# A second FFN's gate and up as seven block products, in three phases instead of one

## The chip, the cores and the metric
The kernel runs on one core of one Trainium2 chip. The metric is the device time of one execution in microseconds; less is better. Engines are called TensorE (PE in the profile, its weight loads PEld), VectorE (DVE), ScalarE (ACT), GpSimd (POOL) and SyncE (SP, which issues DMAs).

## The reference, cut to what matters
One layer: a gated FFN, a mixer, a second gated FFN, each behind a norm with a scale and shift that depend on the sequence (1024 prompt tokens and 8 x 4 sample tokens, model width 1024, hidden width 2816, float32).

```python
h = _modulate(_rms(x, p["ffn1_norm"]), sh1, sc1)
x = x + 0.5 * g1[:, None, :] * _swiglu(h, p["ffn1_w_gate"], p["ffn1_w_up"], p["ffn1_w_down"])
h = _modulate(_rms(x, p["mix_norm"]), sh2, sc2)
m, new = _mixer(h, conv[l], hst[l], shift[l], wkv[l], p)
x = x + g2[:, None, :] * m
h = _modulate(_rms(x, p["ffn2_norm"]), sh3, sc3)
x = x + 0.5 * g3[:, None, :] * _swiglu(h, p["ffn2_w_gate"], p["ffn2_w_up"], p["ffn2_w_down"])
y = _rms(x, final_norm)
# _swiglu: (silu(h @ w_gate) * (h @ w_up)) @ w_down
```

## The kernel before, in words
Activations lie transposed: 8 tiles of 128 features (KD) by T = 1056 tokens. Every float32 operand of a product is split into a high and a low part, and `mm3` (lines 61 to 63) adds three matmuls: high x low, low x high, high x high. Tokens go in pieces CH of 384, 384 and 288 columns. The hidden width is 22 tiles of 128.

**The first FFN** has two phases. In the first, tokens are two pairs (528 columns each, halves of 264 or 266), features are two halves, and gate and up are taken together as the two rows of a 2 x 2 block matrix. `Up.pair` forms the four output blocks of one hidden tile and one pair with seven block products instead of eight, each of 4 x 3 matmuls (tiles pX, pY, pZ, pW); the sums of weights (`summed`) and of activations (`Blocks.sums`, `split_sums`, slots t1 to t4) are made before. Hidden tiles 0 and 1 go plainly with eight (`plain_mm`), to give time for the sums. Hidden tiles are stored to DRAM (dh). At its start come the norm (`pair_rstd`, `pair_norm`), the modulation (`ada8`: matmuls adaps; parts 2 to 8 run behind the products), the scale sc1 (`coeff`, line 160) and the splits. There GpSimd does the sums of blocks and the additions of squares of pair 1. In the second phase `ffn` with dH reads hidden tiles back, splits them and multiplies by w_down in groups of 2 or 3 tiles (GROUPS; psum pd), and VectorE adds the result into x (`acc_x`, line 445).

**The mixer** (projections, two recurrences) ends with a chain of 16 chunks (pd, line 973), with other work as filler in between: at last `w_out` (psum po), two halves of the contraction; the first half for all three token pieces, then the second half piece by piece as the chain delivers, each piece followed by the third norm (`norm3`: squares nsq, sums nacc on VectorE, h).

**The second FFN** is one phase: for each group of hidden tiles gate and up plainly (pg, pu: 8 x 3 matmuls on each of three token pieces), silu, split in SBUF, then down (pd); the last group's down ends piece by piece with the final norm.

The order of instructions on each engine comes from a planner with a simulated timeline, except where `in_order` fixes it; a tile's slot is handed on when its last reader is done. One program order, many queues: DMAs wait in the queue of the engine that issues them.

## Time and profile before

| | |
|---|---|
| time, median of 3 runs | 2252.24 us (2249.97 to 2261.13) |
| the profiled execution | 2250.29 us, of which the span is 2248.5 us |
| TensorE busy | 2153.0 us, 96% |
| VectorE busy | 1219.0 us, 54% |
| ScalarE busy | 647.3 us, 29% |
| GpSimd busy | 208.8 us, 9% |
| moved by DMA | 227.8 MB |

The profiled execution is one run; busy is the time in which at least one instruction of the engine runs. Matmuls are pipelined, so the cost of one is the distance between two starts, not its own duration.

### The profile page before, as it was taken

What the parts mean: (1) busy time and instruction counts of PE and PEld (TensorE: products, weight loads), DVE (VectorE), ACT (ScalarE), POOL (GpSimd) and SP (SyncE); (2) the same over time, 40 slices, a digit from 0 to 9 for tenths busy, and PEclk for the clock granted to TensorE, in tenths of its full rate; (3) what the DMA queues carried; (4) which work ended last, traced back from release to release, by engine and by line L of the source; (5) the groups of instructions that cost most, each with busy time, mean ns of one, the idle gap of its engine ahead of it and who ended that gap; (6) DMA issues with size and microseconds to landing.
All of it is one profiled execution on the core that took longest, in us unless ns stands there. A gap on an engine that the chain in (4) does not pass through costs nothing.

```text
span 2248.5 us, 39509 instructions
## 1 busy us (share of the span) xinstructions
PE 2153.0 (96%) x16633; PEld 2040.1 (91%) x16633; DVE 1219.0 (54%) x2511; ACT 647.3 (29%) x1102; POOL 208.8 (9%) x264
## 2 busy tenths in 40 slices
PE   5899999999999989899898889999999999999997
PEld 4799999999999988798786689899999999999997
DVE  5755555565956576674855666853433333232325
ACT  4433232333312144443332442431111111212123
POOL 3300000000000041214220000000000000000004
PEclk8999999999999999999999899999999999999998
DMA  6244444443623121346476666111111111101112
GB/s 229 95 147 151 138 141 144 136 142 106 237 85 107 56 89 51 97 105 149 115 173 160 180 152 141 40 61 45 48 48 48 38 48 38 57 32 63 38 48 78
DMA packets 135666, 227.80 MB, mean 101 GB/s; under 512 B 74080, under 2 KB 90496, under 8 KB 133440
## 3 DMA queue, kind: packets, MB, share of 16 engines
q1 hardware_dynamic: 74336, 155.71, 21.6%
q10 hardware_dynamic: 49488, 35.45, 6.8%
q0 software_dynamic: 11664, 34.11, 5.3%
q8 instruction: 131, 2.15, 0.4%
q14 instruction: 47, 0.39, 0.1%
HBM read 177.55 MB, written 47.60 MB: 100 GB/s over the span
## 4 chain that ended last, share of the span: by engine, by line
PE 83%; DVE 6%; DMA 4%; ACT 3%; issue 2%; ACTq 1%; POOL 0%; SPq 0%; DVEq 0%; POOLq 0%
PE pd L61 7%; PE pd L63 7%; PE pd L62 7%; PE pg L61 4%; PE pu L61 4%; PE pu L62 4%; PE pu L63 4%; PE pg L63 4%; PE pg L62 4%; PE pX L61 2%; PE pZ L61 2%; PE pW L63 2%; PE pW L62 2%; PE pj L61 2%; PE pX L63 2%
## 5 line engine op out<-in xcount | busy, mean ns | idle before, releaser
L63 PE MATMUL pd<-fh,wh 128*128 128x384 f32 (+1 forms) x1056 | 340.8, 323 | 0.0
L62 PE MATMUL pd<-fh,wl 128*128 128x384 f32 (+1 forms) x1056 | 340.4, 322 | 0.0
L61 PE MATMUL pd<-fl,wh 128*128 128x384 f32 (+1 forms) x1056 | 339.1, 323 | 0.0
L47 DVE TENSOR_TENSOR wl<-wr,wh 128x1024 fp32r<-128x1024 f32 (+1 forms) x206 | 205.4, 999 | 200.6 <-ACT wh L46 199.1
L46 ACT ACTIVATE wh<-wr 128x1024 fp32r<-128x1024 f32 (+1 forms) x206 | 179.8, 875 | 377.4 <-PE pd L63 187.6
L62 PEld LDWEIGHTS pd<-fh,wl 128*128 128x128 f32 x1056 | 198.4, 188 | 0.0
L61 PEld LDWEIGHTS pd<-fl,wh 128*128 128x128 f32 x1056 | 198.3, 188 | 0.0
L63 PEld LDWEIGHTS pd<-fh,wh 128*128 128x128 f32 x1056 | 198.2, 188 | 0.0
L445 DVE SCALAR_TENSOR_TENSOR x<-pd,g3c,x 128x384 f32<-128x384 f32 (+1 forms) x192 | 108.4, 572 | 117.6 <-PE pd L63 117.4
L445 DVE SCALAR_TENSOR_TENSOR x<-pd,g1c,x 128x384 f32<-128x384 f32 (+1 forms) x192 | 107.8, 568 | 81.5 <-PE pd L63 81.4
L482 DVE TENSOR_TENSOR hf<-pu,sg 128x384 f32<-128x384 f32 (+1 forms) x66 | 34.6, 524 | 183.8 <-PE pu L63 182.3
L177 POOL TENSOR_TENSOR nacc<-nacc,nsq 128x384 f32<-128x384 f32 (+1 forms) x35 | 37.5, 1071 | 1007.5 <-ACT nsq L176 1002.3
L46 ACT ACTIVATE fh<-hf 128x384 fp32r<-128x384 f32 (+1 forms) x66 | 32.8, 498 | 216.7 <-DVE hf L482 216.7
L63 PE MATMUL pW<-t,wh 128*128 128x266 f32 (+1 forms) x320 | 91.4, 286 | 0.0
L62 PE MATMUL pW<-t,wl 128*128 128x266 f32 (+1 forms) x320 | 91.3, 285 | 0.0
L61 PE MATMUL pW<-t,wh 128*128 128x266 f32 (+1 forms) x320 | 91.1, 285 | 0.0
L481 ACT ACTIVATE sg<-pg 128x384 f32<-128x384 f32 (+1 forms) x66 | 30.5, 464 | 123.2 <-PE pg L63 121.9
L326 POOL DMA_DIRECT2D dh<-hf x44 | 24.0, 546 | 445.4 <-DVE hf L407 413.3
L146 PE MATMUL adaps<-wa,cT 128*32 128x256 f32 x576 | 48.7, 411 | 14.2 <-DMA wa<-in_w_ada 13.8
L47 DVE TENSOR_TENSOR wl<-s,wh 128x512 fp32r<-128x512 f32 x60 | 45.7, 763 | 28.0 <-ACT wh L46 28.0
L401 ACT ACTIVATE e<-e,bt 128x262 f32<-128x262 f32 (+1 forms) x40 | 20.6, 516 | 139.2 <-DVE bt L400 135.1
L62 PEld LDWEIGHTS pW<-t,wl 128*128 128x128 f32 x320 | 60.3, 189 | 0.0
(531 smaller groups left out, 6065.8 us busy)
## 6 DMA issues: line engine op xcount, KB each, us to landing
wa<-in_w_ada SPq DMA_DIRECT2D x72, 512.0 KB, 4.0
wr<-in_ffn_w_gate SPq DMA_DIRECT2D x44, 512.0 KB, 3.6
wr<-in_ffn_w_up SPq DMA_DIRECT2D x44, 512.0 KB, 3.5
wr<-in_ffn_w_down SPq DMA_DIRECT2D x44, 512.0 KB, 3.5
ch<-dc ACTq DMA_DIRECT2D x32, 576.0 KB, 7.2
dh<-hf POOLq DMA_DIRECT2D x44, 264.0 KB, 2.7
wr<-dh SPq DMA_DIRECT2D x22, 528.0 KB, 4.4
wr<-in_w_in SPq DMA_DIRECT2D x22, 512.0 KB, 3.9
```

The costliest lines, as they stand in the source:

```text
L46: nc.scalar.activation(hi, raw, AF.Copy)
L47: nc.vector.tensor_tensor(lo, raw, hi.bitcast(F32), op=ALU.subtract)
L61: nc.tensor.matmul(ps, wh, xl, start=(first and i == 0), stop=False, **kw)
L62: nc.tensor.matmul(ps, wl, xh, start=False, stop=False, **kw)
L63: nc.tensor.matmul(ps, wh, xh, start=False, stop=(last and i == n - 1), **kw)
L146: nc.tensor.matmul(ps[32 * q:32 * q + 32, :], cT[:, k, :], w[:, 256 * q:256 * q + 256], start=(k == 0), stop=(k == KD - 1), tile_position= ...
L177: adder.tensor_tensor(acc[:, 0:np_], acc[:, 0:np_], sq[:, 0:np_], op=ALU.add)
L326: nc.gpsimd.dma_start(self.dH[m][:, 528 * p:528 * p + 528], hf)
L401: nc.scalar.activation(g2[:, 0:n], g2[:, 0:n], AF.Silu, bias=bt[:, 0:1])
L445: nc.vector.scalar_tensor_tensor(x[:, ob, c:c + np_], ps[:, 0:np_], g[:, ob, 0:1], x[:, ob, c:c + np_], op0=ALU.mult, op1=ALU.add)
L481: nc.scalar.activation(sg, pg, AF.Silu)
L482: nc.vector.tensor_tensor(hf, pu, sg, op=ALU.mult)
```

## The change
- Both FFNs use one function `up_phase` for gate and up by seven products. For the second FFN x comes from DRAM (dX, now two tensors of 528 columns, one for each pair) on GpSimd's queue, hidden tiles go to DRAM, and there is no modulation in it.
- `ffn` becomes `down`, for both; the second FFN's down is a phase of its own that loads x from dX again.
- The norm's factor is multiplied in first (`pair_unit`), the scale sc goes into the split itself (`Blocks.split` with a column), and ScalarE scales the block afterwards for the sums (`pair_scale`). Sums of blocks and of squares move from GpSimd to VectorE. Three buffers take squares in turn.
- `w_out`: the first half of the last token piece moves behind the chain (`w_out_end`), with its weights loaded there again; the norm's root for pair 0 of the second FFN is made before it; x goes to dX piece by piece.
- Stores of x go through GpSimd's queue (`dx_move`), that of p_wkv through SyncE's. The first down phase has 4 weight buffers instead of 3.

```diff
-    def pair_rstd(p, X, ps_, sp, tmp, adder=nc.vector):
+    def pair_rstd(p, of, ps_, sp, tmp):
...
+            sq = tmp[:, 2 * w * (1 + k % 3):2 * w * (2 + k % 3)]
...
-                adder.tensor_tensor(acc, acc, sq, op=ALU.add)
+                nc.vector.tensor_tensor(acc, acc, sq, op=ALU.add)
...
+    def pair_unit(X, p, k, rs):
+        w = PAIRS[p][1]
+        for t, r in zip(prompt(X, p, k), [rs.rearrange("p (j t) -> p j t", j=2)] if p == 0 else [rs[:, 0:w], rs[:, w:NP - 528]]):
+            nc.vector.tensor_tensor(t, t, r, op=ALU.mult)
+
+    def pair_scale(X, p, k, sc):
+        for t in prompt(X, p, k):
+            nc.scalar.activation(t, t, AF.Copy, scale=sc[:, k, 0:1])
...
+            def one(src, h, l):
+                nc.scalar.activation(h, src, AF.Copy, scale=col)
+                nc.vector.scalar_tensor_tensor(l, src, col, h.bitcast(F32), op0=ALU.mult, op1=ALU.subtract)
...
     def w_out():
-        for half in range(2):
...
+        for og in range(2):
+            W = w_load(0, og)
+            if og == 0:
+                yield
+            for ci in range(2):
+                yield from w_block(W, 0, og, ci)
+        W = [w_load(1, og) for og in range(2)]
+        for ci in range(3):
+            c, n = CH[ci]
+            yield min(c + n, NP)
             for og in range(2):
...
+                yield from w_block(W[og], 1, og, ci)
+            if ci < 2:
+                dx_move(nc.gpsimd, c, n, True)
+
+
+    def w_out_end():
+        W = [w_load(0, og) for og in range(2)]
+        for og in range(2):
+            for _ in w_block(W[og], 0, og, 2):
+                pass
+        add_samples(g2c)
+        dx_move(nc.gpsimd, 768, 288, True)
...
+    def up_phase(ph, pre, xsrc, sc, i_sh, left, right, last=(), first=None, second=None, rest=None):
...
+                with in_order(nc.vector), in_order(nc.scalar):
+                    if rest:
+                        r0 = pair_rstd(0, lambda k: X[0][k // 4][:, :, k % 4], WU, spr, slot("a10", F32, "nt"))
+                        next(r0)
+                        W0 = up.plain(*R0)
+                        for rs0 in r0:
+                            pass
+                    else:
+                        rs0 = spread(rn3, WU, spr)
+                        W0 = up.plain(*R0)
+                    for k in range(KD):
+                        pair_unit(X[0], 0, k, rs0)
...
-                    B[0].sums(nc.gpsimd)
...
-            B[1].sums(nc.gpsimd)
+            B[1].sums(nc.vector)
             B[1].split_sums(("e0", "e1", "c1", "x10"))
...
     with ExitStack() as ph:
+        PL_["w"] = PL_["wr"] = opened(ph, "wC", {"wr": 1, "wh": 4, "wl": 4})
+        tmp = opened(ph, "rC", {"nt": 1})
+        r3 = pair_rstd(0, lambda k: x[:, k, 0:528].rearrange("p (j t) -> p j t", j=2), lambda sh, name: P.tile(sh, F32, tag="wu", name=name),
+                       type("R", (), {"tile": staticmethod(lambda sh, dt, tag, name: rn3)}), tmp.tile([128, 2128], F32, "nt", "nt"))
+        for _ in range(2):
+            next(r3)
+        w_out_end()
+    mx.close()
+    PL_["wn"] = T
+    with ExitStack() as ph:
+        up_phase(ph, "ffn2", dX, sc3, 6, ("x10", "x11", "e2", "c1", "x00", "x01", "a10"), ("e0", "e1", "a11", "a12"), ("a00", "c0", "a01", "a02"))
...
-        for _ in ffn("ffn2", h3, g3c, sp, hid, final, pieces=(0, 1, 2), marks=((2, 4), (5, 7))):
+        for _ in down("ffn2", g3c, dH, hid, more, final, hot=True, main_done=yo_pool, marks=((2, 4), (5, 7))):
             pass
```

## Rows read from the trace of the kernel before
**Rows 1.** The page's shares of the chain that ended last, by engine.
```profile
PE 83%; DVE 6%; DMA 4%; ACT 3%; issue 2%; ACTq 1%; POOL 0%; SPq 0%; DVEq 0%; POOLq 0%
```
**Rows 2.** Busy time by stage (us from the span's start; length; busy us and instructions of each engine, TensorE's clock, the DMA engines' share, GB/s): first FFN's start, its products, its down phase, the mixer, the second FFN up to its last matmul of down.
```profile
0.00:108.40 108.40, 75.94 (x568) 64.37 (x569) 66.21 (x113) 45.41 (x88) 37.46 (x25) 0.86 0.46 166
108.40:563.20 454.80, 454.80 (x3814) 423.71 (x3813) 262.15 (x547) 141.66 (x270) 24.86 (x44) 1.00 0.42 138
563.20:830.00 266.80, 262.12 (x1644) 261.15 (x1642) 176.39 (x367) 67.05 (x87) 21.06 (x21) 1.00 0.34 115
830.00:1459.20 629.20, 584.70 (x5773) 515.96 (x5774) 420.47 (x964) 234.58 (x399) 99.84 (x150) 0.96 0.51 123
1459.20:2231.00 771.80, 771.80 (x4822) 771.72 (x4822) 284.48 (x511) 154.98 (x251) 14.22 (x14) 1.00 0.14 47
```
**Rows 3.** The timeline of TensorE in the second FFN (start, duration in us): the first matmuls of up on the last token piece, of the next hidden tile's gate, of a group's down, and of the two hidden tiles after it.
```profile
1646.01 0.30 PE L61 MATMUL pu<-h2l,wh 128*128 128x288 f32 x1
...
1649.23 0.34 PE L61 MATMUL pg<-h0l,wh 128*128 128x384 f32 x1
...
1672.60 0.34 PE L61 MATMUL pd<-fl,wh 128*128 128x384 f32 x1
...
1707.36 0.34 PE L61 MATMUL pg<-h0l,wh 128*128 128x384 f32 x1
...
1730.52 0.34 PE L61 MATMUL pg<-h0l,wh 128*128 128x384 f32 x1
```
**Rows 4.** The same view in the first FFN: the first matmul of hidden tile 2's two pairs and of tile 3, and the first matmul of down.
```profile
108.40 0.28 PE L61 MATMUL pX<-b,wh 128*128 128x266 f32 x1
...
118.79 0.28 PE L61 MATMUL pX<-b,wh 128*128 128x264 f32 x1
...
129.04 0.28 PE L61 MATMUL pX<-b,wh 128*128 128x266 f32 x1
...
563.30 0.29 PE L61 MATMUL pd<-fl,wh 128*128 128x288 f32 x1
```
**Rows 5.** The page's group of the modulation's matmuls over the whole span (busy us, mean ns of one, idle time before them).
```profile
L146 PE MATMUL adaps<-wa,cT 128*32 128x256 f32 x576 | 48.7, 411 | 14.2 <-DMA wa<-in_w_ada 13.8
```
**Rows 6.** DMA issues (queue, number, KB each, median us from issue to landing): the whole span, the first 112 us, 550 to 640 us; the landing times of all moves of dx.
```profile
wr<-in_ffn_w_down SPq DMA_DIRECT2D x44, 512.0 KB, 3.5
dh<-hf POOLq DMA_DIRECT2D x44, 264.0 KB, 2.7
...
x<-in_xT SPq DMA_DIRECT2D x4, 528.0 KB, 5.7
...
x<-in_xT POOLq DMA_DIRECT2D x2, 1536.0 KB, 17.2
x<-in_xT POOLq DMA_DIRECT2D x1, 1152.0 KB, 8.1
dh<-hf POOLq DMA_DIRECT2D x2, 264.0 KB, 12.4
...
DMA to landing us min/median/max: 3.8/6.0/12.0
```
**Rows 7.** The timeline of VectorE in the first FFN's start (start, duration; idle time before it and who ended it).
```profile
28.16 0.23 DVE L160 SCALAR_TENSOR_TENSOR sc<-mod,vec 128x72 f32<-128x72 f32 x1
...
65.59 6.29 DVE L225 SCALAR_TENSOR_TENSOR x<-x,sc,nrs 128x266 f32<-128x266 f32 x16 [0.33 <-ACT nrs L219]
77.06 0.68 DVE L310 TENSOR_TENSOR s<-s,wr 128x512 f32<-128x512 f32 x1
77.66 0.68 DVE L311 TENSOR_TENSOR wr<-wr 128x512 f32<-128x512 f32 x1
...
85.62 2.53 DVE L47 TENSOR_TENSOR t<-x,t 128x1064 fp32r<-128x1064 f32 x1 [3.50 <-ACT t L46]
88.08 5.73 DVE L47 TENSOR_TENSOR wl<-s,wh 128x512 fp32r<-128x512 f32 x2
96.92 1.27 DVE L47 TENSOR_TENSOR t<-x,t 128x1064 fp32r<-128x1064 f32 x1
```
**Rows 8.** Busy time by stretch of the first FFN's start, columns as in rows 2, and the sum over all stretches from 28.50 to 108.40.
```profile
40.00:45.40 5.40, 0.97 (x9) 0.76 (x7) 5.40 (x5) 0.64 (x1) 3.54 (x2) 1.00 0.00 0
45.40:50.00 4.60, 4.60 (x25) 4.60 (x26) 4.16 (x5) 2.48 (x4) 2.72 (x2) 0.63 0.00 0
...
87.40:95.00 7.60, 0.00 (x1) 0.00 (x0) 7.46 (x7) 2.13 (x4) 5.79 (x2) 0.70 0.00 0
95.00:100.60 5.60, 5.53 (x25) 5.53 (x26) 3.12 (x5) 1.89 (x4) 1.27 (x2) 0.50 0.58 182
...
sum 79.90, PE 62.98 PEld 57.81 DVE 57.39 ACT 34.26 POOL 36.67; mean PE 7.00 PEld 6.42 DVE 6.38 ACT 3.81 POOL 4.07
```
**Rows 9.** The mixer's end: busy time of one stretch, columns as in rows 2; all matmuls of the chain's pd (ns min/median/max, first and last start in us).
```profile
1348.00:1405.00 57.00, 57.00 (x547) 51.68 (x547) 37.32 (x87) 11.57 (x21) 1.49 (x2) 1.00 0.60 139
...
L973 PE MATMUL pd<-X,ch x256: 222/222/369, 1207.2 to 1436.7; 128*64 128x64 f32 x128
```
**Rows 10.** The timeline of VectorE at the mixer's end.
```profile
1442.05 0.55 DVE L177 TENSOR_TENSOR nacc<-nacc,nsq 128x384 f32<-128x384 f32 x1
...
1443.63 0.62 DVE L445 SCALAR_TENSOR_TENSOR x<-po,mod,x 128x384 f32<-128x384 f32 x1
...
1448.69 0.69 DVE L47 TENSOR_TENSOR h2ly<-o,h2hy 128x512 fp32r<-128x512 f32 x1 [0.61 <-ACT h2hy L46]
```

More of the change, by code (lines that the diff above doesn't have):

```diff
@@ L306, in summed @@
             g1, g2, u1, u2 = G[:, 0:512], G[:, 512:], U[:, 0:512], U[:, 512:]
-            s1, s2, s4 = (self.sm.tile([128, 512], F32, "s", "s") for _ in range(3))
+            s1, s2, s4 = (self.sm.tile([128, 528], F32, "s", "s")[:, 0:512] for _ in range(3))
             tt = nc.vector.tensor_tensor
@@ L490, in ffn @@
                 main_done()
-            from_ = (more, more) if more and GROUPS.index((g0, g1)) % 2 == 0 else (hid, PL_["w"])
-            def hid_load(m):
+            from_ = (more, more) if gi % 2 == 0 else (hid, PL_["w"])
+            hid_t, wd = [], []
+            for m in range(g0, g1):
                 r = PL_["wr"].tile([128, T], F32, "wr", "wr")
@@ L1309, in trunk, with dx_move @@
     g2c = mod[:, 40:48, :]
-    dX = dram.tile([128, KD, T], F32, name="dx")
-    def hid_pool(ph):
-        return ph.enter_context(tc.tile_pool(name="hid", bufs=3, side="right", reuse_waits="tile"))
+    rn3 = const.tile([128, 6], F32, name="rn3")
+    dX = [dram.tile([128, KD, 528], F32, name=f"dx{p}") for p in range(2)]
+    def dx_move(queue, c, n, store, k0=0, k1=KD):
+        for p in range(2):
+            b, e = max(c, 528 * p), min(c + n, 528 * p + 528)
+            if e > b:
+                s, d = x[:, k0:k1, b:e], dX[p][:, k0:k1, b - 528 * p:e - 528 * p]
+                queue.dma_start(*((d, s) if store else (s, d)))
     def norm_pool(ph):
@@ L1357, in trunk @@
                 load_x(0)
-                r0 = pair_rstd(0, X[0], WU, spr, slot("a10", F32, "nt"))
-                for rs0 in r0:
-                    pass
-                for _ in ada8(1, PY, sp, stage):
-                    pass
-                R0 = up.raw(0)
+                R0 = up.raw(0)
+                if rest is None:
+                    R1 = up.raw(1)
+                with in_order(nc.vector), in_order(nc.scalar):
[10 more added lines that the diff above has]
+                        pair_unit(X[0], 0, k, rs0)
+                if first:
+                    first(sp, stage)
                 load_x(1)
-                R1 = up.raw(1)
-                ada0 = ada8(0, PY, sp, stage)
-                coeff(sc1, 1, V_N1)
+                if rest is not None:
+                    R1 = up.raw(1)
+                late = second(sp, stage) if second else iter(())
                 B[0] = Blocks(0, X[0], slot, ("a00", "a01", "a02", "c0"))
@@ L1444, in trunk, with first, rest @@
             pass
+    def first(sp, stage):
+        for _ in ada8(1, PY, sp, stage):
+            pass
+        coeff(sc1, 1, V_N1)
+    def rest(sp, own):
+        for i in range(2, 9):
+            yield from ada8(i, PY, sp, own)
+            if i == 2:
+                nc.scalar.activation(g1c, mod[:, 16:24, :], AF.Copy, scale=0.5)
+            if i == 4:
+                coeff(sc2, 4, V_NM)
+            if i == 8:
+                coeff(sc3, 7, V_N2)
+                nc.scalar.activation(g3c, mod[:, 64:72, :], AF.Copy, scale=0.5)
+    fx, mx = es.enter_context(ExitStack()), es.enter_context(ExitStack())
+    PL_["wr"] = opened(fx, "wrp", {"wr": 3}, side="right")
+    with ExitStack() as ph:
+        up_phase(ph, "ffn1", [xT[:, :, 528 * p:528 * p + 528] for p in range(2)], sc1, 0,
+                 ("a10", "e0", "e1", "x10", "a11", "a12", "c1", "x01", "a00", "x11", "e2", "c0", "a01", "a02", "x00"), (), (),
+                 first, lambda sp, stage: ada8(0, PY, sp, stage), rest)
     hp = None
-    xt = es.enter_context(tc.tile_pool(name="xp", bufs=1, reuse_waits="tile")).tile([128, KD * XW], F32, tag="x", name="x")
+    xt = mx.enter_context(tc.tile_pool(name="xp", bufs=1, reuse_waits="tile")).tile([128, KD * XW], F32, tag="x", name="x")
     x = xt.rearrange("p (k t) -> p k t", k=KD)
```

238 lines of the change are left out of this document (98 added, 140 removed).

## The prediction, on record before the result

> **What bounds the kernel now.** The page first: TensorE is busy for 96% of the span, and the chain that ended last lies on it for 83% [rows 1]. That share is a mean, so the table by stage comes next [rows 2]. From 1459 to 2231 us, the second FFN, TensorE has no idle time at full clock, while VectorE, ScalarE and the DMA engines are far from full: what is taken from its matmuls there shows in the end time one for one. The first FFN's products (108 to 563 us) are as full, and so is its down phase until its last group. Not full are the first 108 us (76 busy, clock 0.86) and the mixer (585 of 629). So two questions decide: how much TensorE time the new product scheme saves, and what the two new seams (mixer to FFN, products to down) and the rewritten start of the first FFN cost.
>
> **The saving.** The starts of matmuls show one hidden tile's gate and up of the second FFN, 144 matmuls, take 23.37 us once and 23.16 us once [rows 3]; mean 23.27, for 22 tiles 511.9 us. The same work by seven products is in this trace already, in the first FFN: the first pair takes 118.79 - 108.40 = 10.39 us for 84 matmuls of 266 columns, the second 129.04 - 118.79 = 10.25 us for 84 of 264 [rows 4], together 20.64 us. Tiles 0 and 1 stay plain, with 96 matmuls of each width at 10.39 / 84 = 0.124 us and 10.25 / 84 = 0.122 us: 23.6 us each. New gate and up: 20 x 20.64 + 2 x 23.6 = 460.0 us. Saved: 51.9 us. An eighth of the work would be 64 us; it is less because two tiles stay plain and because a 266-column matmul takes 0.124 us where its share of a 384-column one (0.174 to 0.177) would be 0.122.
>
> Does the rest keep that pace? In the first FFN's stage VectorE is busy 262 of 455 us and the DMA engines 42%, with the modulation's matmuls (7/9 of 48.7 us = 38 us) in between [rows 2, 5]. 20 x 20.64 + 38 = 451 of 455 us: no room for hidden waits. In the second FFN the modulation is absent, so the other engines have about 21 us a tile instead of 23 and VectorE still has a third to spare. I cost it at nothing.
>
> **Down as its own phase.** Down's matmuls stay: three tiles take 1707.36 - 1672.60 = 34.76 us, 22 take 254.9 [rows 3]. New are 22 reads of the hidden tiles and a ScalarE and a VectorE pass on each; the first FFN's down does just this with TensorE busy 262 of 267 us [rows 2]. The tail after the last matmul of down (2231 to the span's end at 2248.5) stays. At the seam, the first tiles to be split lie on the slot of the block that the very last product reads (x00 is both t4 of pair 0 and the first of the new pools). So TensorE waits for two ScalarE passes of about 1 us, a VectorE pass of 1.27 [rows 7] and the hand-overs: 4 us. Bounds: 0, since the first FFN goes over at 563.30 with TensorE idle neither before nor behind [rows 2, 4], and 8.1, the landing of the first x there [rows 6], were x late. I take 4.
>
> **Mixer's end.** Eight blocks of 12 matmuls (first half of w_out, last token piece) move behind the chain. A 288-column matmul is 3.22 / 24 = 0.134 us [rows 3], so 12.9 us. At 1348 to 1405 TensorE is full [rows 9], so taking them out of the filler can shorten the chain by up to 12.9 us; where the chain waits on latency it shortens by nothing. The last blocks of the second half wait for the final split at 1448.69 + 0.69; VectorE loses the third norm's additions before it (0.55 us each, four after 1437), say 2 us [rows 10]. So the matmuls of w_out end at 1447 + 12.9 + 12.9 = 1473 without chain gain, 1460 with the full one; I take 1468.
> Behind this lies the round trip of x. The last x piece that pair 0 needs is done near 1444 [rows 10]. Storing it to DRAM takes 4 to 6 us (dx moves land after 3.8 to 12), loading pair 0 about 6 to 10 (5.7 us for 528 KB) [rows 6], eight multiplications 8 x 0.62 = 5 (512 columns take 0.60 from start to start) [rows 7], the first split 0.6: about 1444 + 20 = 1464, under the 1468. The four added w_out loads go through one buffer, 3.5 us + about 2.5 us of split each: 24 us if they start at 1440, so the last one is there at 1464, when the second group of blocks is due. I let the first matmul of FFN 2 start at 1470; bounds 1460 and 1482.
>
> **The start of FFN 2.** TensorE has 47.2 us of plain work. Pair 1 needs x of the last piece, stored only after 1468: store 4, load 9, squares and sums 5.5, root and spreading 4, 16 multiplications 5.6, splits: first block about 29 us after the start, while TensorE has work for 23.4. A wait of 5, another 2 for the tail split (128 columns of samples after the second half's splits), 1 for the rest. VectorE's own sum is tight: tile 0's weights 2.4, pair 0 5.0 + 5.8, tile 1's weights 2.4, the seven sums of squares 4.4, pair 1 5.6 + 6.2, samples 2, two outputs 3.3, four block sums 4.8 and their splits 4.8, tile 2's weights 6.6, in all 53 us by the uncontended rows (0.60 for 512 columns, 0.39 for 266, 1.2 for 1064) [rows 7], in some 55 us. After a gap TensorE runs at 1.2 instead of 2.4 GHz: 4.6 us at 0.63 after a gap of 4.4, 5.6 us at 0.50 after one of 7.5 [rows 8]: 2 us lost. Sum 10; bounds 4 and 28 (what the old first start lost, below).
>
> **The start of FFN 1** changes too: the norm no longer waits for the scale, it goes into the split, and the additions on GpSimd (block sums, squares of pair 1) move to VectorE. Before, from the scale at 28.16 us to the first product at 108.40 are 80.2 us; the work in it is 47.2 plain and 8 steps of modulation at 48.7 / 72 = 0.68 [rows 5], 5.4; 27.6 remain, lost but for a small norm. The windows show where: 0.97 busy of 5.4 us, nothing in 7.6 us, and two stretches at 0.50 and 0.63 of the clock [rows 8]. In the second gap VectorE crawls while GpSimd adds: 2.53 us for a split that takes 1.27 later, 5.73 us for two that take 0.68 each alone [rows 7].
> The Trainium skill, SBUF — State Buffer, "Who interferes with whom", says that a VectorE operation with two SBUF inputs and a GpSimd operation that reads SBUF exclude each other for the whole instruction. The trace agrees (5.73 beside 0.68); by that rule alone about 6 us come back, and without it the additions could also stay slow on VectorE, which would make the sum about 14 us higher.
> After the change VectorE's new work (7 x 0.62 + 8 x 1.2 = 14 us) fits: it was idle 22 of these 80 us [rows 8], and most of its 7.5 busy us in the second gap were contention. I take 20 of the 27.6 us back; bounds 0 and 26.
>
> **Sum**, on the profiled run (span 2248.5, run 2250.3, so 1.8 around it; the median of the runs shown is 2252.2): 1470 + 460.0 + 10 + 4 + 254.9 + 17.5 = 2216.4, less 20 = 2196.4, plus 1.8 = **2198**.
>
> **Rivals.**
> *The first start gives nothing* (VectorE, with 14 us more, becomes its bound): 2218. For it: VectorE is busy 57 of the 80 us there [rows 8].
> *The round trips through DRAM are exposed.* Moves on GpSimd's queue land much later in the busy stretch at 550 to 640 us: 12.4 us for a hidden tile against 2.7 over the whole run, 8.1 and 17.2 for x [rows 6]. Then pair 0 starts at 1444 + 12.4 + 17.2 + 6 = 1480 (+10), pair 1 is some 12 later than planned, and half clock adds 2: 2222. Against it: little else moves on the DMA engines then (47 GB/s in the second FFN) [rows 2].
> The Trainium skill, same page, "SBUF: two separate sides", warns that GpSimd's queue cannot write descriptors while VectorE runs in a two-port mode; that would give this rival's time. No row here shows it.
> *The seven products save nothing here:* a tile takes 23.3 us again, because VectorE or the loads fall behind; then 20 x 2.6 = 53 are back: 2251. Against it: the 455 us above.
> *Slower: the planner's new order hurts the mixer's chain.* The order of every queue comes from a simulated timeline, and pools, queues and filler of the mixer change. 16 chunks take 1207 to 1437 us, 14.4 each [rows 9]; from 4.1 us more per chunk on (66 in all) the kernel is slower by over 0.5%; at 5 us it is 2278. Against it: the filler only shrinks.
>
> **Numbers.** Chances: forecast 0.58, first start 0.16, round trips 0.12, no saving 0.07, chain 0.07. 0.5% (11 us, 2241 to 2263) is about what a measurement of this kernel can tell from no change; the first three are faster: 0.86; same 0.07, slower 0.07. The forecast's own range is 2180 to 2216, from its bounds (start 1460 to 1482, stalls 4 to 28, first start 26 to 8) taken not all at once. The range 2176 to 2232 takes in the two rivals above it and leaves out the last two.
>
> **What would show it.** First product pair of FFN 1 at 85 to 92 us; a pair in FFN 2 of 10.2 to 10.4 us and 20 tiles in 413; first gate matmul of FFN 2 about 907 us after the first down matmul of FFN 1 (1459.2 - 563.3 = 896 before) and its first product 57 us later, with under 10 us idle in between; a gap of about 4 us before the first down matmul. The prediction is wrong if TensorE idles more than 30 us in these seams, or if those 907 us are more than 930.

## The result, and the profile after

The changed kernel takes 2242.4 us (median of 19 runs, 2232.0 to 2250.7) against 2254.6 for the kernel before beside it: a ratio of 0.9947, 95% interval 0.9936 to 0.9958. It is faster by 0.5%, the forecast was 2.4%. The profiled execution took 2240.2 us with a span of 2238.4, against 2250.3 and 2248.5 before; both are single executions, 2 and 4 us under the medians, and so are all lengths of stages below.

The page of the changed kernel, busy time of each engine and the chain that ended last by engine (before: 96% and [rows 1]):

```profile
PE 2113.9 (94%) x17209; PEld 2000.5 (89%) x17209; DVE 1409.3 (63%) x2954; ACT 734.1 (33%) x1283; POOL 212.2 (9%) x314
...
PE 74%; DVE 9%; DMA 5%; issue 4%; ACT 4%; ACTq 1%; POOL 1%; DVEq 0%; POOLq 0%
```

TensorE lost 39 us of work and the span lost only 10: the rest has become idle time, and the chain now runs over VectorE and DMAs more often. Where it sits is in the table by stage of the changed kernel, cut as [rows 2] and once more at FFN2's first gate matmul (1480.3), its first product (1545.5) and its first down matmul (1959.6):

```profile
core 0: us, PE busy (x) PEld busy (x) DVE busy (x) ACT busy (x) POOL busy (x), PEclk, DMA share, GB/s
0.00:104.10 104.10, 76.54 (x568) 65.51 (x569) 67.64 (x130) 57.35 (x114) 2.07 (x10) 0.90 0.48 172
104.10:558.40 454.30, 454.30 (x3815) 423.29 (x3814) 262.06 (x547) 141.91 (x270) 24.92 (x44) 1.00 0.42 138
558.40:825.00 266.60, 263.49 (x1648) 263.08 (x1647) 175.55 (x366) 67.03 (x87) 20.87 (x22) 0.99 0.34 113
825.00:1480.30 655.30, 588.95 (x5785) 521.46 (x5784) 415.28 (x953) 222.53 (x381) 108.14 (x159) 0.94 0.54 134
1480.30:1545.50 65.20, 55.20 (x408) 53.83 (x409) 55.21 (x103) 44.58 (x89) 4.21 (x8) 0.93 0.24 83
1545.50:1959.60 414.10, 411.54 (x3363) 411.36 (x3361) 261.86 (x535) 137.80 (x262) 26.35 (x46) 1.00 0.24 82
1959.60:2220.00 260.40, 259.74 (x1609) 258.31 (x1610) 161.96 (x309) 58.94 (x75) 14.26 (x14) 0.99 0.31 101
```

The two stages of products and the down phase are full at full clock, as they were to be. The three that are not full are the first start, the mixer with its end (66 us idle, 44 before), and the start of the second FFN. Set against the forecast, stage by stage (us of span; the forecast's 2196.4 and the measured 2238.4 are the sums):

```
stage                                               forecast  measured  difference
start to FFN1's first product                          88.4     104.1     +15.7
FFN1's products                                       454.9     454.3      -0.6
FFN1's first down matmul to FFN2's first gate matmul  906.7     921.9     +15.2
that to FFN2's first product                           57.2      65.2      +8.0
FFN2's products, to its first down matmul             416.8     414.1      -2.7
down and the tail                                     272.4     278.8      +6.4
```

### The profile page after: what moved, and what is told of

Its sections match the earlier page's. It is cut to its first block, busy times and chain, and to the rows that moved or that the text cites. A ratio compares the mean times of both kernels' runs of the same rounds, so it can differ in the third digit from the quotient of the medians.

```text
span 2238.4 us, 41844 instructions
## 1 busy us (share of the span) xinstructions
PE 2113.9 (94%) x17209; PEld 2000.5 (89%) x17209; DVE 1409.3 (63%) x2954; ACT 734.1 (33%) x1283; POOL 212.2 (9%) x314
## 4 chain that ended last, share of the span: by engine, by line
PE 74%; DVE 9%; DMA 5%; issue 4%; ACT 4%; ACTq 1%; POOL 1%; DVEq 0%; POOLq 0%
PE pd L61 7%; PE pd L62 7%; PE pd L63 7%; PE pX L61 4%; PE pZ L61 4%; PE pX L62 3%; PE pZ L63 3%; PE pX L63 3%; PE pW L61 3%; PE pW L63 3%; PE pW L62 3%; PE pZ L62 3%; PE pY L63 2%; PE pY L61 2%; PE pY L62 2%
## 5 line engine op out<-in xcount | busy, mean ns | idle before, releaser
L46 ACT ACTIVATE wh<-wr 128x512 fp32r<-128x512 f32 (+1 forms) x254 | 192.3, 761 | 249.9 <-PE pZ L63 71.7
L47 DVE TENSOR_TENSOR wl<-wr,wh 128x512 fp32r<-128x512 f32 (+1 forms) x254 | 215.1, 851 | 87.5 <-ACT wh L46 82.1
L61 PE MATMUL pW<-t,wh 128*128 128x266 f32 (+1 forms) x640 | 182.6, 285 | 0.0
L63 PE MATMUL pW<-t,wh 128*128 128x266 f32 (+1 forms) x640 | 182.3, 285 | 0.0
L62 PE MATMUL pW<-t,wl 128*128 128x266 f32 (+1 forms) x640 | 182.2, 285 | 0.0
L419 ACT ACTIVATE e<-e,bt 128x262 f32<-128x262 f32 x80 | 41.3, 516 | 293.4 <-DVE bt L418 273.8
L46 ACT ACTIVATE fh<-wr 128x1056 fp32r<-128x1056 f32 x44 | 47.6, 1082 | 246.5 <-PE pd L63 195.9
L62 PEld LDWEIGHTS pW<-t,wl 128*128 128x128 f32 x640 | 120.8, 189 | 0.0
L61 PEld LDWEIGHTS pW<-t,wh 128*128 128x128 f32 x640 | 120.5, 188 | 0.0
L63 PEld LDWEIGHTS pW<-t,wh 128*128 128x128 f32 x640 | 120.5, 188 | 0.0
L47 DVE TENSOR_TENSOR wl<-s,wh 128x512 fp32r<-128x512 f32 x120 | 82.7, 690 | 58.5 <-ACT wh L46 58.5
L416 DVE TENSOR_TENSOR e<-pZ,e 128x266 f32<-128x266 f32 x80 | 34.5, 431 | 104.3 <-PE pZ L63 104.1
L46 ACT ACTIVATE wh<-s 128x512 fp32r<-128x512 f32 x120 | 75.4, 629 | 68.4 <-PE pW L63 31.4
```

What stands on the lines that cost most here:

```text
L46: nc.scalar.activation(hi, raw, AF.Copy)
L47: nc.vector.tensor_tensor(lo, raw, hi.bitcast(F32), op=ALU.subtract)
L61: nc.tensor.matmul(ps, wh, xl, start=(first and i == 0), stop=False, **kw)
L62: nc.tensor.matmul(ps, wl, xh, start=False, stop=False, **kw)
L63: nc.tensor.matmul(ps, wh, xh, start=False, stop=(last and i == n - 1), **kw)
L416: tt(g2, pz, u, op=ALU.add)
```

## The experiments

Three terms had to be explained, the two starts and the way from the first down matmul to the second FFN ("the mixer's way" below). Line numbers are those of the changed kernel. The figures of all runs stand in one table at the end of this section.

**One part of the change undone: w_out's last piece.** The first half's last token piece goes back between the chunks:

```diff
-            for ci in range(2):
+            for ci in range(3):
                 yield from w_block(W, 0, og, ci)
...
-        W = [w_load(0, og) for og in range(2)]
-        for og in range(2):
-            for _ in w_block(W[og], 0, og, 2):
-                pass
         add_samples(g2c)
```

> The changed kernel with one part of the change undone: all three token pieces of the first half of w_out lie between the mixer's chain steps again, as before, and nothing of w_out is left behind the chain but the adds. Theory (the chain is bound by its own latency, so filler inside it is free and filler behind it is paid in full): the last chain product comes as late behind the first FFN's first down product as in the changed kernel (874 us), the first gate product of FFN2 comes some 19 us earlier (903 us behind that product where the changed kernel has 922), and the time falls by 15 to 25 us against the changed kernel, to about 2217 to 2227. Rival (TensorE bounds the chain, and moving the products out of it shortens it): the chain ends about 13 us later (887 us), the first gate product stays near 920 us, and the time stays within 5 us of 2242.

Measured: 0.9917 (0.9896 to 0.9938), 2235.6 us. The chain's last product is 872.8 us behind the first down matmul (874.3 in the changed kernel), so in this pair moving the blocks out had not shortened the chain. That is a hint that TensorE does not bound it and no proof: in the same comparison of the runs below it is 872.9 moved and 873.2 back (e2, e4), but 880.9 and 889.6 in e6 and e8, and over all the kernels with the change the chain ends between 868 and 890 us. The gate matmul came only 5 us earlier, not 19. The rest of the lateness has another source. One part of it is seen at the end of w_out, in the changed kernel and in this one:

```profile
1472.81 0.29 PE L63 MATMUL po<-h2hy,wh 128*128 128x288 f32 x1
1480.32 0.59 PE L61 MATMUL pg<-b,wh 128*128 128x264 f32 x1 [7.22 <-DVE b L276]
```
```profile
1463.40 0.29 PE L63 MATMUL po<-h2hy,wh 128*128 128x288 f32 x1
1463.53 1.02 PE L223 MATMUL npb<-ident,rn 88*128 88x88 f32 x8
1471.05 0.56 PE L61 MATMUL pg<-b,wh 128*128 128x264 f32 x1 [6.50 <-DVE b L276]
```

In both TensorE waits some 7 us for the first split block. VectorE's rows of the changed kernel say what comes first there: the last additions of w_out, then tile 0's weights, then the norm's multiplications, then the split.

```profile
1474.22 0.42 DVE L473 TENSOR_TENSOR x<-x,sacc 128x256 f32<-128x256 f32 x1
1474.77 0.27 DVE L476 MEMSET sacc<- 128x256 f32 x1
1474.96 2.43 DVE L47 TENSOR_TENSOR wl<-wr,wh 128x512 fp32r<-128x512 f32 x4
1477.30 2.56 DVE L236 TENSOR_TENSOR x<-x,nrs 128x528 f32<-128x528 f32 x4
1479.78 1.70 DVE L276 SCALAR_TENSOR_TENSOR b<-x,sc,b 128x264 fp32r<-128x264 f32 x4
```

In the kernel before, the second FFN's first gate matmuls ran *between* the last matmuls of w_out, 5.7 us ahead of its end, because the first token pieces were done and in SBUF:

```profile
1459.16 0.34 PE L61 MATMUL pg<-h0l,wh 128*128 128x384 f32 x1
...
1464.84 0.30 PE L63 MATMUL po<-h2hy,wh 128*128 128x288 f32 x1
```

Now they come 7.5 us behind it. Splitting tile 0's weights after the multiplications was not tried.

**Was the mixer's old length something to build on?** Two edits of the kernel *before* that touch no line of the mixer, each a single piece of the change:

```diff
-                r1 = pair_rstd(1, X[1], WU, spr, slot("a10", F32, "nt"), nc.gpsimd)
+                r1 = pair_rstd(1, X[1], WU, spr, slot("a10", F32, "nt"))
```
```diff
-            B[1].sums(nc.gpsimd)
+            B[1].sums(nc.vector)
```

> The kernel before with only the sums of pair 1's squares moved from GpSimd to VectorE, in the first FFN; no line of the mixer is touched, but the planner lays the mixer out anew. Theory (the layout of the mixer before was a lucky one, and any edit ahead of it costs): from FFN1's first down product to FFN2's first gate product 905 to 918 us instead of 895.9, the first product 2 to 8 us earlier than 108.4, and the time 2250 to 2268. Rival (the 17 us that the run with all sums on VectorE lost there have to do with those sums): 893 to 899 us, and the time 2245 to 2252.

> The kernel before with only pair 1's block sums moved from GpSimd to VectorE; the mixer's lines are untouched, its layout by the planner is new. Theory (lucky layout before): from the first down product to FFN2's first gate product 905 to 918 us, and the time 2250 to 2268. Rival: 893 to 899 us, time 2245 to 2252.

Ahead of them a run with both edits and pair 0's sums as well:

> The kernel before with one part of the change alone: the block sums of both pairs and the sums of pair 1's squares run on VectorE instead of GpSimd, in the first FFN. My step for the first FFN's start (which gave 20 of 27.6 us back for the end of the contention between GpSimd and VectorE): the first product at 88 to 95 us instead of 108.4, and the time 2235 to 2242. Rival (the order of the work, not the engine, sets the start): the first product at 102 to 108 us and the time within 7 us of 2254, lower by the 4 us that the changed kernel gained.

The mixer's way in the kernel before, and in these two:

```profile
563.30:1459.20 895.90, 846.72 (x7416) 0.97 0.46 120
```
```profile
561.00:1469.90 908.90, 850.38 (x7415) 0.96 0.45 119
```
```profile
560.50:1473.00 912.50, 859.04 (x7416) 0.95 0.45 118
```

(Columns: window, length, TensorE busy, its clock, the DMA engines' share, GB/s.) The same matmuls take 13 and 17 us longer, and 17 us with all three edits (912.9). Part is idle time, part is lower clock, and with it longer busy time. All three starts got shorter (by 2.3, 2.8 and 8.3 us), and yet the kernels are slower or no faster: 1.0032 (1.002 to 1.0043), 1.0038 (1.0023 to 1.0052) and 0.9998 (0.9985 to 1.0011). Some of the 13 and 17 us is the luck of the profiled executions: by the medians, with the shorter starts added back, what comes behind the start got longer by 10, 11 and 9 us, which is still more than the intervals allow. The order did change: of the some 7400 matmuls of the mixer's way, TensorE runs only the first 1836 in n3 and the first 2365 in n4 in the order of the kernel before. So the 895.9 us were one draw of the planner (one of many orders in which it can lay out the same work), and a good one; each of the three edits ahead of the mixer drew again.

n4 also shows what the contention between GpSimd and VectorE cost at the start. The two weight splits and the activation split that took 5.73 and 2.53 us before [rows 7] take 0.67 each and 1.25 with pair 1's sums on VectorE (rows of n4; line numbers of the kernel before), and TensorE's wait for the silu of tile 0 falls from 7.67 us (first row below, the kernel before) to 3.17 (second row, n4). Yet the first product comes only 2.8 us earlier.

```profile
86.38 1.25 DVE L47 TENSOR_TENSOR t<-x,t 128x1064 fp32r<-128x1064 f32 x1
87.56 0.67 DVE L47 TENSOR_TENSOR wl<-s,wh 128x512 fp32r<-128x512 f32 x1
...
89.34 0.67 DVE L47 TENSOR_TENSOR wl<-s,wh 128x512 fp32r<-128x512 f32 x1
```
```profile
95.07 0.59 PE L61 MATMUL pu<-b,wh 128*128 128x266 f32 x1 [7.67 <-ACT e L362]
```
```profile
93.40 0.59 PE L61 MATMUL pu<-b,wh 128*128 128x266 f32 x1 [3.17 <-ACT e L362]
```

In e5_before_sums_dve the first product came at 100.1, between the 88 to 95 expected and the rival's 102 to 108.

**Draws on the side of the changed kernel.** As e1_chain_fill, with one number of the configuration changed; no work is added or left out.

```diff
-CFG = dict(... foff=5, ... pre=5, st=2)
+CFG = dict(... foff=5, ... pre=4, st=2)    # v3; v6: pre=6; v5: st=3; v4: foff=3
```

> The changed kernel with the third token piece back in the filler (as in e1_chain_fill), and one number of the filler changed: 4 steps of the linear recurrence ahead of the chain's first chunk instead of 5. Nothing is added or left out; only the layout of the mixer is drawn anew. Theory (the mixer's length between FFN1's first down product and FFN2's first gate product is a matter of the layout, worth some 15 us either way): this distance moves by 3 to 15 us against the 916.8 of e1_chain_fill, up or down, and the time moves with it (2222 to 2250). Rival (the layout is settled by the work in it): within 2 us of 916.8 and 2235.6.

> As the run before, with 6 steps of the linear recurrence ahead of the chain instead of 5. Theory: the distance moves by 3 to 15 us from 916.8, up or down, and the time with it. Rival: within 2 us of both.

> As e1_chain_fill, with the mixing of the linear recurrence into the samples' steps beginning one step later. Theory: the distance moves by 3 to 15 us from 916.8, up or down, and the time with it. Rival: within 2 us of both.

> As e1_chain_fill, with the rotation of the PSUM banks for the products begun at another place (3 instead of 5), which changes the order in which banks come free from the first down phase on. Theory: the distance moves by 3 to 15 us from 916.8, up or down, and the time with it. Rival: within 2 us of both.

The mixer's way became 912.0, 922.2, 921.7 and 910.5 us, and the times 2230.6, 2239.9, 2242.6 and 2226.2 (0.9893, 0.9932, 0.9930 and 0.9866, intervals of 0.0016 to 0.003 either side). The theory of the draw holds: 12 us between kernels of the same work, and the times of the shortest and the longest (v4, v6) lie apart beyond their intervals.

What in a layout makes the difference was not settled as a whole. One place of the changed kernel shows the kind:

```profile
1260.44 0.33 PE L968 MATMUL py<-X,ch 64*64 64x64 f32 x4
1266.65 1.52 PE L937 MATMUL pw<-ch 128*64 128x64 f32 x16 [5.88 <-issue]
```
```profile
1261.47 0.55 DVE L1003 SCALAR_TENSOR_TENSOR late<-x,vec 128x32 f32<-128x32 f32 x2 [3.07 <-DMA x<-x]
...
1265.67 0.42 DVE L956 TENSOR_TENSOR St<-pd,pc 128x256 f32<-128x256 f32 x1
1266.13 0.87 DVE L960 TENSOR_TENSOR ch<-St,Sd 64x256 f32<-64x256 f32 x2
```

The chain's step St could go when pd is done, before 1258. It stands on VectorE's queue behind twelve instructions of the samples' work, the first of which waits for a small DMA; TensorE stands still for 5.9 us and goes on when `ch` is written (the view names no releaser, "issue"). A kernel with this wait alone taken away was not tried; what it costs stays open.

**The starts: three orders.** In the changed kernel VectorE puts pair 0's block sums (L294) between the sums of pair 1's squares (L206), and TensorE waits for the last of these:

```profile
46.02 1.26 DVE L294 TENSOR_TENSOR x<-x,x 128x1056 f32<-128x1056 f32 x1 [0.20 <-ACT x L240]
47.19 0.71 DVE L206 TENSOR_TENSOR nt<-nt 128x532 f32<-128x532 f32 x1
47.82 1.25 DVE L294 TENSOR_TENSOR x<-x,x 128x1056 f32<-128x1056 f32 x1
48.99 0.70 DVE L206 TENSOR_TENSOR nt<-nt 128x532 f32<-128x532 f32 x1
49.61 1.25 DVE L294 TENSOR_TENSOR x<-x 128x1056 f32<-128x1056 f32 x1
50.78 1.52 DVE L206 TENSOR_TENSOR nt<-nt 128x532 f32<-128x532 f32 x2
```
```profile
52.36 1.92 PE L210 MATMUL nps<-ones,nt 128*88 128x1 f32 x12 [2.64 <-DVE nt L206]
```

First order: all scaling behind the last split.

```diff
+                    with tc.issue_after(last_on(nc.scalar)[0]):
                         for p in (1, 0):
                             for k in range(KD):
                                 pair_scale(X[p], p, k, sc)
```

> The changed kernel with the activations' scaling by the norm, of both pairs, held back until ScalarE has split the last tail of the token block, in both FFNs' starts; the block sums that read the scaled pairs follow. Theory (pair 0's scaling and sums, put ahead of pair 1's squares, keep TensorE's norm products waiting on VectorE): the wait of the norm products on VectorE's squares shrinks from 14 us to under 5, FFN1's first product comes at 88 to 95 us instead of 104.1, FFN2's first product 57 to 62 us behind its first gate product instead of 68, and the time falls by 12 to 25 us against the changed kernel, to about 2217 to 2230. Rival (VectorE's sum of work bounds the start in any order): the first product stays within 4 us of 104.1 and the time within 5 us of 2242.

The wait of pair 1's norm products (2.64 us above; the 14 us of the expectation are the wait of pair 0's norm from the start of the span, which stays, and its 68 us were 65.2) is gone, and the silu of tile 0, now behind 11.4 us of scaling on ScalarE, holds TensorE for 9.3 us instead of 3.2:

```profile
92.16 0.59 PE L61 MATMUL pu<-b,wh 128*128 128x266 f32 x1 [9.34 <-ACT e L380]
```

First product at 104.4, FFN2's 66.2 us behind its gate matmul, 0.9931 (0.9914 to 0.9948): nothing gained. With the filler put back as well (its distance 919.5), the same, 0.9936 (0.9912 to 0.996):

> Both edits of the two runs above at once. If both theories hold, their gains add up: 2190 to 2205. If only the filler counts, about 2220; if only the order of the scaling counts, about 2222; if neither, 2242.

Second order: pair 0's scaling and sums directly behind pair 1's squares, pair 1's scaling behind the first silu.

```diff
                     next(r1)
+                    for k in range(KD):
+                        pair_scale(X[0], 0, k, sc)
+                    B[0].sums(nc.vector)
...
                         up.plain_out(u, ps, kept[:, T * u:T * u + T])
+                        if u == 0:
+                            with tc.issue_after(last_on(nc.scalar)[0]):
+                                for k in range(KD):
+                                    pair_scale(X[1], 1, k, sc)
```

> The changed kernel with another order in both FFNs' starts: pair 0's scaling and block sums come behind pair 1's squares and their sums (VectorE and ScalarE are nearly idle in the ten us after those), pair 1's scaling behind the first silu of tile 0. Theory (the order made the stall, and holding the scaling back in one block only moved it): no wait of the norm products on VectorE over 1 us, and none over 4 us before the second tile's products, so FFN1's first product at 93 to 97 us (104.1 in the changed kernel), FFN2's first product 55 to 60 us behind its first gate product (65.2). The time 2222 to 2232. Rival (the planner's new order of the mixer takes back what the starts give): the starts as said, but from FFN1's first down product to FFN2's first gate product 925 to 935 us instead of 921.9, and the time within 6 us of 2242.

> The order of the starts of the run before and the third token piece of w_out's first half back in the chain's filler. Theory: both starts as there, from the first down product to FFN2's first gate product 914 to 918 us, the time 2215 to 2225. If the mixer's plan takes the gain back: 2230 to 2240.

The first product came at 98.5 and 96.4, but a new wait stood right behind it, in both FFNs, and the products took 461.2 us instead of 454.3:

```profile
104.59 0.59 PE L61 MATMUL pY<-t,wh 128*128 128x266 f32 x1 [4.51 <-DVE t L47]
```

The mixer's ways were 929.8 and 925.0, the first as the rival had it, and the times 0.9989 (0.9974 to 1.0003) and 0.9961 (0.9946 to 0.9976): the first is slower than the changed kernel by 0.4%, which neither theory nor rival had, and the second gains nothing on it. Was VectorE full, or did the norm come too late? The norm of pair 1 earlier in TensorE's order (`if k == 0: next(r1)`, `if k == 1: rs1 = next(r1)`, instead of 1 and 3), alone and with the second order, on the version with the filler put back (g3 and f3 with `foff=3` as in v4_foff3, f5 with 5):

> As v4_foff3, with the norm of pair 1 taken earlier in TensorE's order in both starts: its sums over features behind the first step of tile 1's products instead of the second, its spreading behind the second instead of the fourth (some 4.5 us of other TensorE work ahead of VectorE's work on pair 1 less). Theory (VectorE's work on pair 1 starts when the norm is spread, and everything up to the first product hangs on that): FFN1's first product 3 to 6 us earlier than the 101.9 of v4_foff3, FFN2's first product 60 to 63 us behind its first gate product instead of 65.2, and the time 2214 to 2222 if the mixer's layout keeps its 910.5. Rival (the squares' sums are not ready earlier, so TensorE waits there instead): both within 1.5 us of the values of v4_foff3.

> As the run before, with the order of e6_start_order as well (pair 0's scaling and sums behind pair 1's squares, pair 1's scaling behind the first silu). Theory: the squares are then ready in time, FFN1's first product at 91 to 95 us, and the 4.5 us that TensorE waited behind it in e6_start_order shrink below 1.5; FFN2's first product 56 to 59 us behind its first gate product. The time 2200 to 2212 with a layout as in v4_foff3. Rival (VectorE is full from the norm to the first products, and what is pulled ahead is waited for behind): the first product at 91 to 95, but over 4 us of waiting within the 15 us behind it, and FFN1's products 459 us or more instead of 454.

> As the run before with the rotation of the PSUM banks as in the changed kernel (5), so another layout of the mixer. Theory: the same starts as there, within 2 us, and a distance from FFN1's first down product to FFN2's first gate product that differs by 3 to 15 us from that run's; the time differs by as much.

Alone the norm only waits longer (4.6 us instead of the 1.4 of v4_foff3; first product 104.7; 0.9935, 0.9914 to 0.9955). With the second order the first product came at 96.0 and 97.0 (0.9945, 0.9923 to 0.9967, and 0.9925, 0.9901 to 0.9948), and the wait behind it was 4.53 us in both, 4.51 before, though the norm was spread 2 to 3 us earlier (second half at 55.8 and 56.9 us, 59.0 in e6_start_order). By its marks on record (over 4 us of waiting, products of 459 us or more) the rival of a full VectorE came in. But a wait that does not shrink when VectorE's work may begin earlier points at another cause, the place of pair 1's scaling: the first products are pair 1's, and they need its sums first. So, as a test, the third order pulls only pair 0 ahead and leaves pair 1 where the change has it (with the early norm):

```diff
-                    for p in (1, 0):
-                        for k in range(KD):
-                            pair_scale(X[p], p, k, sc)
+                    for k in range(KD):
+                        pair_scale(X[1], 1, k, sc)
```

> As f5_order_norm, but only pair 0's scaling and sums are pulled ahead; pair 1's scaling is back where the changed kernel has it, ahead of the first silu. Pair 1's blocks are the first that the products need, and f5_order_norm had put them last. Theory (the 4.5 us wait behind the first product came from that, not from a full VectorE): no wait over 1.5 us within 15 us behind the first product, FFN1's products 454 to 456 us long, the first product at 94 to 98 us, FFN1's first down product at 548 to 553 (558.4 in the changed kernel); FFN2's first product 59 to 63 us behind its first gate product and its products 414 to 415 us. The time 2215 to 2235, by the layout drawn. Rival (VectorE's work is the limit): the first product at 100 us or later, or the wait behind it stays at 4 us.

> The same starts with the rotation of the PSUM banks of v4_foff3. By the theory the starts as in h5_pair0_early within 2 us; the distance from FFN1's first down product to FFN2's first gate product between 905 and 926, as it is drawn; the time between 2208 and 2232.

> The same starts with a third rotation of the PSUM banks. By the theory the starts as in h5_pair0_early within 2 us, the distance anywhere between 905 and 926, the time between 2208 and 2232.

No wait behind the first product, and products of 454.2 to 454.3 us: against f5_order_norm, h5_pair0_early moves nothing but pair 1's scaling, so that place made the wait, and not VectorE's sum of work. The first product came at 102.0, 98.3 and 97.0. The 102.0 misses the 94 to 98 expected and meets the rival's other mark (100 or later), and the three differ by more than the 2 us allowed; the order of their starts is the same on every computing engine, and the last section shows what moved them. The start of the second FFN did not get shorter (65.2 to 65.9): there TensorE still waits 2.8 us for the squares, its idle time fell from 10.0 us to between 6.7 and 8.1, but its clock fell too, from 0.93 to between 0.85 and 0.88. The three draws of the mixer gave 912.3, 915.1 and 902.9 us, the times 2225.7, 2227.3 and 2218.4 us: 0.9867 (0.9846 to 0.9888), 0.9867 (0.9851 to 0.9883) and **0.984 (0.9819 to 0.9862)**. The last beats the changed kernel by 1.1%, mostly by its draw: of the 25 us of span between the two profiled executions 19 lie in the mixer's way and 7 in the first start. Paired by layout, the third order shows no gain in h3_pair0_early (2227.3 against 2226.2 of v4_foff3) and 10 us in h5_pair0_early (2225.7 against 2235.6 of e1_chain_fill), so what it is worth by itself is not shown. The profiled execution of h0_pair0_early, the fastest of four:

```profile
0.00:97.00 97.00, 73.20 (x568) 63.27 (x569) 67.94 (x130) 58.19 (x115) 2.06 (x10) 0.93 0.51 184
...
820.00:1454.20 634.20, 583.74 (x5773) 516.43 (x5771) 409.64 (x947) 226.11 (x382) 105.38 (x158) 0.95 0.55 134
1454.20:1520.10 65.90, 57.84 (x408) 56.76 (x409) 55.62 (x103) 44.42 (x89) 4.20 (x8) 0.88 0.25 82
```

All runs, from their profiled executions (us; the mixer's way is that from the first down matmul to FFN2's first gate matmul; times are medians):

```
run                    1st product  products  mixer's way  gate to product    time
before                    108.4      454.9       895.9           -           2254.6
e5_before_sums_dve        100.1      454.9       912.9           -           2255.1
n3_before_squares_dve     106.1      454.9       908.9           -           2263.0
n4_before_sums1_dve       105.6      454.9       912.5           -           2263.2
the changed kernel        104.1      454.3       921.9         65.2          2242.4
e1_chain_fill             100.1      454.2       916.8         66.2          2235.6
e2_scale_after_split      104.4      454.3       921.8         66.2          2239.0
e4_both                   105.2      454.3       919.5         66.3          2240.0
e6_start_order             98.5      461.2       929.8         62.0          2253.0
e8_order_and_fill          96.4      461.2       925.0         61.3          2247.2
v3_pre4                   101.8      454.3       912.0         65.1          2230.6
v6_pre6                   104.5      454.3       922.2         65.5          2239.9
v5_st3                    104.4      454.3       921.7         67.7          2242.6
v4_foff3                  101.9      454.2       910.5         65.2          2226.2
g3_norm_early             104.7      454.3       924.9         66.4          2240.3
f3_order_norm              96.0      461.2       925.8         62.7          2245.6
f5_order_norm              97.0      461.3       914.5         62.1          2236.4
h5_pair0_early            102.0      454.2       912.3         65.2          2225.7
h3_pair0_early             98.3      454.3       915.1         65.6          2227.3
h0_pair0_early             97.0      454.3       902.9         65.9          2218.4
```

## Why the prediction was wrong

**The saving** was right. Twenty tiles of FFN2 take 414 us including the seam (forecast 416.8), the other engines keep pace, and the round trips of hidden tiles and of x are hidden: x of pair 0 was there 25 us before it was used (its loads issued from 1438 to 1444, 7.9 us in the median to landing, the multiplications at 1477), so the rival of exposed round trips is refuted for pair 0. For pair 1 no engine waits for a load of x (stored at 1474.9, loads issued from 1481.7, squares from 1491.5 behind other work of ScalarE). Late landings on GpSimd's queue come at the seam to down, 15.7 us for a hidden tile and 18.5 for a piece of x; the hidden tile holds ScalarE for 10.9 us, but TensorE's only wait of note there is 2.56 us for VectorE's split, where the step had 4. Whether the Trainium skill's warning about GpSimd's queue (SBUF — State Buffer, "SBUF: two separate sides") has a part in these two landings, no row shows.

**Mixer's end** failed, +15.2 us. The step took the length of the mixer in the trace before, 895.9 us, as a base and added 11 for the change. The base does not carry over: with the mixer's lines untouched it is 909 to 913 us after three small edits elsewhere, 13 to 17 more, or 9 to 11 by the medians. From 909 to 913 the change added 9 to 13, near the 11 forecast, but not by the terms forecast. The gate matmul comes 7.5 us behind w_out's end instead of the 2 forecast, where it had come 5.7 ahead of it; this part stands clear of the draws (7.4 to 7.9 behind in all sixteen kernels with the change, 5.7 to 6.4 ahead in the four without). The moved blocks cost 2 to 5 us, not 12.9 less a gain (921.9 to 916.8, 921.8 to 919.5 and 929.8 to 925.0 where they are put back), each read within the spread of the draws. These two make 15 to 18, more than the 9 to 13; what gave the rest back is open. So is how much of the 15.2 is the draw: in the changed kernel's own trace the chain's last product comes where it did before (874.3 and 873.4 us behind the first down matmul), and the whole lateness of 26 us lies behind it. With the draw of h0_pair0_early, 902.9 us, the same step would have looked right. The possible shortening of the chain, bounded by 12.9, does not show in the pairs above. The rival "the planner's new order hurts the mixer's chain" named the right mechanism with a wrong place and price: it wanted a fixed sum per chunk and got 0.07, though each of these edits drew the whole layout anew. Its argument against, "the filler only shrinks", speaks of work, not of order.

**The start of FFN 1** failed, +15.7 us: 4.3 came back where 20 were forecast. The step took the contention away and held that VectorE's new work fits into its idle time. The idle time is at the wrong places: in the changed kernel VectorE is busy for 0.28 us between 53 and 62 us, while the norm travels, and what the planner pulled into the squares ahead of that held up the norm itself. The same edits on the kernel before gave 8.3 us for all sums and 2.3 and 2.8 for single ones, in single executions, and the one wait that the contention held up fell by 4.5 us in n4. So the contention is worth between the 4.5 us of that wait and the 8.3 of the whole start, in which the clock has a part; the rest of the 20 was not contention. The Trainium skill's rule (SBUF — State Buffer, "Who interferes with whom") had given about 6 us in the prediction; the trace agrees with the page (5.73 us for two splits beside 0.67 each once pair 1's sums are off GpSimd). TensorE from the first gate matmul to the first product:

```profile
31.96:104.10 72.14, 63.84 (x476) 0.88 0.33 119
```

52.6 of the 63.8 busy us are the work of the forecast, and the waits are 8.3 us. Of the other 11, the half clock makes at most 8.7 (the clock is 0.88), and the norm's matmuls, left out as small, 3.6 (partly the same time). The forecast left 7.6 for all of this from 28.2 us on, of which 3.8 were over at the first gate matmul. Order is not the whole of it either: the third order reached 97.0 to 102.0, not 88.4, and that rest stays open. The rival "the first start gives nothing" had nearly the size, but its reason, VectorE as the bound, does not fit: VectorE is busy 67.6 of the 104.1 us.

**The start of FFN 2** failed in the same way, +8.0: 18 us beyond the 47.2 of work where 10 were allowed. 10.0 are idle time, 3.6 of it for pair 1's squares and 3.2 for the silu, with the same interleaving; 8.0 are the norm's matmuls and a clock of 0.93. That VectorE's work there, 53 us by rows (55.2 measured), is close to the whole start was in the text; it was costed as a sum and not as an order.

**Down** failed by 6.4 us. The price per tile came from groups of three, 254.9 us for 22 tiles; with gate and up, 511.9, that makes 766.8 of a stage that took 771.8 [rows 2, 3]. The missing 5 us were visible, and the first FFN's down phase, 267 us, was the nearer row.

The time lies outside the range (2176 to 2232), and yet neither of the two signs of being wrong appeared: TensorE idles 20 us at the seams, not 30, and the 907 us became 921.9, not 930. The signs leave out the first start, and they leave room for errors that add up.

## What to carry to other kernels

Where a planner lays out all queues at once, as here, the length of an untouched stage in the old trace is one draw, and that of one execution besides: try some layouts of nothing (a filler count, a bank rotation) on either side before crediting an edit with one or two per cent, and give a forecast that spread. A stall that ends on a busy engine can be one of order, as in these starts: moving work out of its way pays only if what it was moved behind is not needed sooner, so ask which block the next matmul reads first. Check that the terms read from parts of a stage add up to the stage.

## What the hardware showed that was not expected

The same gap does not always cost the same. In h5_pair0_early and h0_pair0_early TensorE waits 3.16 and 3.15 us for the same silu, with the same work behind it; in the first the clock is down afterwards, in the second it stays full (windows of h5 and of h0; columns: window, length, TensorE busy, clock, DMA share, GB/s):

```profile
80.00:90.00 10.00, 6.84 (x50) 0.88 0.14 54
90.00:100.00 10.00, 10.00 (x67) 0.77 0.14 54
```
```profile
80.00:90.00 10.00, 6.84 (x56) 1.00 0.31 108
90.00:100.00 10.00, 10.00 (x84) 1.00 0.18 52
```

The matmul behind the wait, in the one and the other:

```profile
88.45 0.59 PE L61 MATMUL pu<-b,wh 128*128 128x266 f32 x1 [3.16 <-ACT e L380]
```
```profile
86.17 0.39 PE L61 MATMUL pu<-b,wh 128*128 128x266 f32 x1 [3.15 <-ACT e L380]
```

So the first product of one and the same start (the same instructions in the same order on every computing engine) fell between 100.1 and 104.5 us (e1, v3, v4, the changed kernel, v5, v6) and between 97.0 and 102.0 (h0, h3, h5) in single executions. The granted clock goes with it. From 40 us to the first product of e1, the changed kernel, h5, h3 and h0:

```profile
40.00:100.10 60.10, 52.71 (x430) 0.97 0.24 87
40.00:104.10 64.10, 55.80 (x424) 0.89 0.24 83
40.00:102.00 62.00, 56.67 (x430) 0.89 0.23 84
40.00:98.30 58.30, 53.14 (x428) 0.94 0.25 90
40.00:97.00 57.00, 52.32 (x430) 0.97 0.26 91
```

A start with gaps near three us can't be forecast to better than these 4 to 5 us from one trace. Why the clock falls in one execution and not in the next stays open.
